# A list scheduler's table of durations: TensorE passes at traced issue times, and a shared way into SBUF for VectorE and GpSimd

## The chip, the core and the metric

One core of one Trainium2 chip runs the whole program. The metric is the device time of one execution in microseconds (us). The kernel before ran three times: 3467.73, 3470.81 and 3473.10 us, median 3470.81 us. One more execution was profiled, and all rows below are from it.

## What is computed

Two transformer blocks one after the other, all in 32-bit floats, for 512 tokens (and 256 context tokens in the first block) of width 1024:

```python
for li in range(2):                                   # the first block
    h  = half_ffn(h, ...); hc = half_ffn(hc, ...)     # h + 0.5 * gate * (silu(z @ Wg) * (z @ Wu)) @ Wd
    y, yc = even_mixer(...) if li == 0 else odd_mixer(...)   # attention beside a gMLP, or beside pooling
    h = h + m[5] * y
    h = half_ffn(h, ...)                              # and hc again in layer 0
# the second block: one projection, gated delta rule in chunks, three sliding windows, gates, output
```

`half_ffn` has an inner width of 2816, that is 22 column blocks of 128. The factors `m` come from a modulation, a product of one vector per condition with a 1024 x 9216 matrix per layer ("ada" in the program's names).

## The kernel before

Every product with full inputs is made from three TensorE passes: each operand is split into a high and a low half (`halves`: ScalarE copies the value into the narrower type, VectorE or GpSimd subtracts), and high x high, high x low and low x high are summed in one bank. In names, `whi` and `wlo` are the halves of weights, `zh` and `zl` those of the tokens, `ah` and `al` those of the activations. `raw` is a weight tile as loaded, 128 x 1024.

An FFN (`ffn`, with `gate_up`, `swiglu` and `down` in it) runs over the 22 column blocks f. For each f, gate and up of all tokens come from seven products of sums of blocks in place of eight: GpSimd makes two sums into new tiles `ws` and three in place (`raw<-raw`), ScalarE and VectorE split seven tiles of 128 x 512 (GpSimd takes the subtraction of one of them), TensorE runs 7 x 12 = 84 passes "gu", and VectorE adds the products up, multiplies gate and up and splits the result (`al`). After every second f the down projection of a pair of blocks runs (`dn`, 6 passes of 512 columns for each of 12 halves of token tiles, or of 8), and VectorE adds it to `h`. There are three FFNs with six token tiles (384 columns in a "gu" pass) and, last in the first block, one with four tiles (256 columns). In the group of column blocks before the last one, each half of a tile of `h` is also multiplied by the gate (VectorE, `h<-h,gate`) and the residual is added (GpSimd, `h<-h,hin`). At the end of an FFN or an output projection, `scaled` takes the rows' root mean square (GpSimd raises to a power: `rr<-ms`), VectorE scales (`xn<-h,rr`), TensorE transposes (`tr`), VectorE and ScalarE scale and shift (`h<-tr,mods`), and `combine` makes the sums and halves that the next FFN multiplies (`zs`, `zh`, `zl`, `zxh`, `zxl`).

The order in which each engine gets its instructions is not written by hand. `Program.record` notes every instruction with its inputs, a rank (phase, stream, place as written) and what `cost` says of it: how long it holds its engine and how much later its result is there. `Program.order` then plays a list scheduler: it keeps a clock for each of the five engines; an engine takes the first by rank among the instructions that can start at its clock (or within WAIT = 0.12 us of it, for all but TensorE); results reach another engine after the lag plus SLACK = 0.26 us, or SLACK_PE = 0.7 us for TensorE; a tile's place in its pool has to be free. Between engines, the earliest start goes next, and at equal times the engine that stands first in ENGINES (tensor, vector, scalar, gpsimd, sync). What comes out is emitted as five fixed queues: on the chip each engine works its queue in order and waits at semaphores for real inputs only. So `cost` changes no instruction and no wait, only places in the queues. Every instruction is issued from one line, the `getattr` in `emit`: L602 before, L619 in the change, so rows tell groups apart by tile names. Of `cost`, one line gives TensorE's passes with split operands:

```python
return max(n / 2400, 0.107) + 0.0027, 0.1
```

Of the kernel before, what the change touches and what calls it, by code (L numbers as in the profile page):

```python
# [175 lines left out]
class View:  # L176
    """A part of a tile: what an instruction will read or write once the tile has a place."""
# [69 lines left out]
    def cells(self):  # L247
        """The partitions and, as bits, the pieces of each that the view covers."""
# [20 lines left out]
class Slot:  # L269
    """A tile to be: its place in a pool is taken by its first instruction and given back by its last."""  # L270
# [43 lines left out]
# What the order of the instructions leaves for guesses that prove too short, in us: how much later than its inputs an  # L314
# instruction of TensorE, or one of another engine, is taken to start; and how long an engine waits for a better one.
# [3 lines left out]
# Banks of PSUM that the first stream leaves to the one behind it.  # L319
# [29 lines left out]
class Op:  # L349
    __slots__ = ("eng", "fn", "args", "kw", "key", "phase", "deps", "users", "takes", "gives", "left", "ready",  # L350
                 "cost", "lag", "n", "t")
# [12 lines left out]
def cost(eng, fn, args, kw, n):  # L364
    """About how long an instruction holds its engine, and how much later its result is there, in us."""
# [4 lines left out]
    if eng == "tensor":  # L370
        if fn == "transpose":
            return 0.109, 0.1
        lhs, rhs = args[1], args[2]
        if rhs.dtype == F32:
            c = max(4 * n / 2400, 0.213) + 0.005
            if "tile_position" in kw:
                c /= 3.8
            elif lhs.shape[-1] == 64:
                c *= 0.63
            return c, 0.1  # L380
        return max(n / 2400, 0.107) + 0.0027, 0.1
# [14 lines left out]

class Program:
    """Instructions in the order in which they are written down, each with a rank, and the order in which the engines
    are to have them: each engine takes the first by rank among those that can start."""
# [20 lines left out]
    def record(self, eng, fn, args, kw):  # L420
# [7 lines left out]
        op.cost, op.lag = cost(eng, fn, args, kw, n)  # L428
        for v, w in [(v, False) for v in ins] + [(v, True) for v in out]:
# [19 lines left out]
    def order(self):  # L449
# [50 lines left out]

        def place(o):
            r = o.ready
# [21 lines left out]
        while len(out) < len(ops):  # L524
# [18 lines left out]
            clock[o.eng] = end  # L543
            out.append(o)
# [64 lines left out]
class Net:  # L609
# [40 lines left out]
    def split(self, v, eng=None, pool=None):  # L650
        """The two parts of each v[:, i]."""
# [12 lines left out]
    def halves(self, hi, lo, x, eng=None):  # L664
        """x as the sum of two parts, each of which one pass carries."""
        self.nc.scalar.copy(hi, x)
        (eng or self.nc.vector).tensor_sub(lo, x, hi.bitcast(F32))
# [25 lines left out]
    def proj_t(self, cols, ws):  # L693
        """Tokens on partitions: the tokens of z in cols times the columns of ws."""
# [5 lines left out]
    def proj_f(self, w, t0, n):  # L700
        """Features on partitions: 128 features times n tokens of z."""
# [6 lines left out]
    def turn(self, src, n=4):  # L708
        """n blocks of 128 columns, each with its rows and columns exchanged."""
# [13 lines left out]
    def ada(self, li, n):  # L723
        self.ada_end()
        """512 columns of a layer's modulation: of half of one of its nine vectors, for both conditions. Its last steps
        are left for ada_end."""
# [67 lines left out]
    def scaled(self, h_t):  # L794
        """The halves of a tile of h, each row over its root mean square."""
# [22 lines left out]
    def park(self, i, h, xs, ab=None):  # L818
        """The scaled halves xs of pair i of the tiles of h, rows and columns exchanged, in their place; without ab,
        what ab will scale."""  # L820
# [13 lines left out]
    def park_again(self, h, half, li, ni):  # L834
        """Scales half of the rows of what waits parked, all tokens at once."""
# [8 lines left out]
    def operands(self, zx, n):  # L844
        """What the seven products of swiglu take of z, n tokens each, by parts."""
# [10 lines left out]
    # The operands that take the place of a block of z, and what each of the others sums.  # L856
# [3 lines left out]
    def blocks(self, h, t):  # L860
        """The blocks of z for pair t of the tiles that wait in h."""
# [3 lines left out]
    def plan(self, how):  # L865
        """What a string of operands, each with the letter of an engine, says."""
# [3 lines left out]
    def summed(self, z, i, eng):  # L870
        """Operand i, whole, as a sum of blocks of z: in the place of one of them, or of its own."""
# [8 lines left out]
    def combine(self, t, h, zx):  # L880
        """The operands for the tokens of the parked pair at place t."""
# [8 lines left out]
    def combine_first(self, h, zx):  # L890
        """Those of all tokens, for which the second half of the rows is scaled last."""
# [40 lines left out]
    def gate_up(self, li, which, f, how="gggggg"):  # L932
        """The seven sums of blocks of the gate's and the up's columns f, and their parts, in the order of use."""
# [19 lines left out]
    # The blocks of gate (0, 1) and up (2, 3), by halves of the tokens, that each product adds to or is taken from.  # L953
    USES = (((0, 1), (3, 1)), ((2, 1), (3, -1)), ((1, 1), (3, 1)), ((0, 1), (2, 1)), ((0, -1), (1, 1)), ((3, 1),), ((0, 1),))

    def swiglu(self, ws, z, n, ah, al, order=(1, 3, 2, 4, 0, 6, 5)):
        """silu(gate) * up for n tokens of each half, from seven products of blocks in place of eight."""
# [17 lines left out]
    def ffn(self, li, which, nt, F, hsrc, filler, on_tile, first=None):  # L975
        """hsrc + gate * swiglu(z): the sum grows in F.h."""
# [74 lines left out]
    def gelu2(self, dst, ps):  # L1051
        """Twice the gelu of ps."""
# [8 lines left out]
    def softmax(self, M, scs, widths, sink=None):  # L1061
        """exp(s - max) / sum over the parts of the scores of a pair of heads; parts are (bank of head 0, of head 1)."""
# [31 lines left out]
    def times_v(self, M, Ps, vs, dst):  # L1094
        """dst = v^T P^T for a pair of heads; vs gives v by key tile and head."""
# [153 lines left out]
    def odd_mixer(self, M, units):  # L1249
# [24 lines left out]
        def heads(c):  # L1274
            """What attention takes of half of the heads, a tile of tokens at a time."""
# [119 lines left out]
    def silu2(self, dst, y):  # L1395
        """Twice the silu of y."""
# [430 lines left out]
def at(t, nt):  # L1827
    """Where a tile of tokens is for swiglu: those of a pair at the same place of the two halves."""
# [176 lines left out]
```

## Time and profile before

| | |
|---|---|
| median of three runs | 3470.81 us |
| lowest and highest | 3467.73, 3473.10 us |
| span of the profiled execution, first to last instruction | 3465.6 us |
| the execution's own total | not listed beside its span |
| instructions | 48809 |
| TensorE (PE) busy | 3305.0 us, 95% |
| VectorE (DVE) busy | 2553.9 us, 74% |
| ScalarE (ACT) busy | 1406.0 us, 41% |
| GpSimd (POOL) busy | 1321.4 us, 38% |
| mean DMA share | 29.3% of 16 engines |

The span is 5.2 us under the median of the runs. A busy share is an average over stages: the FFN middles, the starts and ends of FFNs, the mixers and the second block have different limits, and the table of stretches in the rows below is what tells them apart. PE's passes are pipelined, so the length of one row in a timeline is longer than the step from one pass to the next; the step is the difference of two start times.

### The profile page before, as it was taken

What the parts mean: (1) busy time and instruction counts of PE and PEld (TensorE: products, weight loads), DVE (VectorE), ACT (ScalarE), POOL (GpSimd) and SP (SyncE); (2) the same over time, 40 slices, a digit from 0 to 9 for tenths busy, and PEclk for the clock granted to TensorE, in tenths of its full rate; (3) what the DMA queues carried; (4) which work ended last, traced back from release to release, by engine and by line L of the source; (5) the groups of instructions that cost most, each with busy time, mean ns of one, the idle gap of its engine ahead of it and who ended that gap; (6) DMA issues with size and microseconds to landing.
All of it is one profiled execution on the core that took longest, in us unless ns stands there. A gap on an engine that the chain in (4) does not pass through costs nothing.

```text
span 3465.6 us, 48809 instructions
## 1 busy us (share of the span) xinstructions
PE 3305.0 (95%) x18310; PEld 2826.1 (82%) x18310; DVE 2553.9 (74%) x4229; ACT 1406.0 (41%) x2962; POOL 1321.4 (38%) x1032
## 2 busy tenths in 40 slices
PE   6999998999999999989999988998999899999999
PEld 4879997776678999858999978867888787788987
DVE  7678778767777888888887786558999976555433
ACT  4433333544343333344334334445444443234331
POOL 4334435411343444554443353116555543333000
PEclk9999999999999999999999999998999999999999
DMA  5442123231433212242122132343332341112231
GB/s 209 137 160 74 56 74 115 89 128 56 173 127 136 73 56 73 85 168 91 56 73 73 65 123 80 113 158 104 100 102 92 118 122 43 31 49 74 82 98 61
DMA packets 161532, 337.73 MB, mean 97 GB/s; under 512 B 12256, under 2 KB 57696, under 8 KB 161168
## 3 DMA queue, kind: packets, MB, share of 16 engines
q1 hardware_dynamic: 161296, 334.61, 29.3%
q8 instruction: 144, 2.36, 0.3%
q14 instruction: 92, 0.75, 0.1%
HBM read 316.69 MB, written 17.87 MB: 97 GB/s over the span
## 4 chain that ended last, share of the span: by engine, by line
PE 38%; DVE 13%; issue 2%; ACT 1%; POOL 1%; DMA 1%; SPq 0%; ACTq 0%; DVEq 0%; POOLq 0%
PE gu L602 9%; PE pj L602 8%; PE dn L602 5%; DVE wlo L602 4%; PE pjf L602 4%; DVE h L602 3%; DVE gu L602 2%; DVE al L602 2%; PE dmm L602 2%; PE dnp L602 1%; PE fin L602 1%; PE yb L602 1%; PE p L602 1%; PE tr L602 1%; PE sc L602 1%
## 5 line engine op out<-in xcount | busy, mean ns | idle before, releaser
L602 DVE TENSOR_TENSOR wlo<-raw,whi 128x512 fp32r<-128x512 f32 x797 | 670.0, 867 | 197.8 <-ACT whi L602 173.2
L602 ACT CAST whi<-raw 128x512 fp32r<-128x512 f32 x885 | 523.8, 620 | 501.5 <-DMA raw<-in_ffn_gu 116.2
L602 DVE TENSOR_TENSOR gu<-gu 128x384 f32<-128x384 f32 (+1 forms) x880 | 469.1, 564 | 211.4 <-PE gu L602 172.8
L602 POOL TENSOR_TENSOR ws<-raw 128x512 f32<-128x512 f32 x176 | 249.1, 1420 | 828.8 <-DVE gu L602 596.5
L602 ACT ACTIVATE gu<-gu 128x384 f32<-128x384 f32 (+1 forms) x528 | 242.2, 474 | 504.8 <-DVE gu L602 343.4
L602 POOL TENSOR_TENSOR raw<-raw 128x512 f32<-128x512 f32 x264 | 430.6, 1655 | 2.0 <-DVE wlo L602 0.6
L602 PE MATMUL gu<-zh,wlo 128*128 128x384 f32 (+1 forms) x1408 | 300.3, 335 | 55.7 <-DVE wlo L602 54.9
L602 PE MATMUL dn<-whi,ah 128*128 128x512 f32 x968 | 308.3, 397 | 0.2 <-DVE adaSs L602 0.2
L602 DVE TENSOR_TENSOR h<-h,dn 128x512 f32<-128x512 f32 x404 | 269.6, 679 | 52.0 <-PE dn L602 49.2
L602 PE MATMUL dn<-wlo,ah 128*128 128x512 f32 x968 | 307.8, 396 | 0.0
L602 PE MATMUL dn<-whi,al 128*128 128x512 f32 x968 | 307.5, 396 | 0.0
L602 PEld LDWEIGHTS gu<-zh,wlo 128*128 128x128 f32 x1408 | 241.0, 195 | 79.7 <-DVE wlo L602 78.7
L602 PE MATMUL gu<-zh,whi 128*128 128x384 f32 (+1 forms) x1408 | 289.5, 328 | 15.8 <-ACT zh L602 11.2
L602 PE MATMUL gu<-zl,whi 128*128 128x384 f32 (+1 forms) x1408 | 293.0, 328 | 1.2 <-DVE zl L602 1.2
L602 PEld LDWEIGHTS gu<-zh,whi 128*128 128x128 f32 x1408 | 239.9, 192 | 38.1 <-ACT zh L602 14.4
L602 POOL TENSOR_TENSOR rr<-ms,constA 128x4 f32<-128x4 f32 (+3 forms) x112 | 109.4, 980 | 377.5 <-DVE ms L602 362.2
L602 PEld LDWEIGHTS gu<-zl,whi 128*128 128x128 f32 x1408 | 241.9, 193 | 4.1 <-DVE zl L602 2.0
L602 DVE TENSOR_TENSOR wlo<-ws,whi 128x512 fp32r<-128x512 f32 x176 | 220.9, 1269 | 4.8 <-ACT whi L602 3.3
L602 PE MATMUL gu<-zxh,wlo 128*128 128x384 f32 (+1 forms) x1056 | 219.3, 327 | 3.0 <-DVE wlo L602 2.8
L602 PE MATMUL gu<-zxh,whi 128*128 128x384 f32 (+1 forms) x1056 | 214.7, 328 | 7.8 <-ACT whi L602 6.4
L602 ACT CAST whi<-ws 128x512 fp32r<-128x512 f32 x176 | 108.6, 618 | 270.7 <-PE dn L602 227.1
L602 PEld LDWEIGHTS dn<-whi,al 128*128 128x128 f32 x968 | 182.8, 189 | 42.1 <-DVE al L602 0.3
(359 smaller groups left out, 6040.6 us busy)
## 6 DMA issues: line engine op xcount, KB each, us to landing
raw<-in_ffn_gu SPq DMA_DIRECT2D x176, 512.0 KB, 5.2
raw<-in_ada_w SPq DMA_DIRECT2D x144, 512.0 KB, 4.6
raw<-in_ffn_w_down SPq DMA_DIRECT2D x88, 512.0 KB, 3.5
raw<-in_w_in SPq DMA_DIRECT2D x72, 512.0 KB, 3.7
raw<-in_od_w_in SPq DMA_DIRECT2D x16, 512.0 KB, 3.6
raw<-in_ev_w_in SPq DMA_DIRECT2D x14, 512.0 KB, 3.8
gate<-gate SPq DMA_DIRECT2D x10, 512.0 KB, 3.8
raw<-in_ev_w_out SPq DMA_DIRECT2D x8, 512.0 KB, 5.2
```

The lines of the kernel that those rows point to most:

```text
L602: getattr(self.real[o.eng], o.fn)(*[real(x) for x in o.args], **{k: real(v) for k, v in o.kw.items()})
```

## The change

A TensorE pass on split operands is planned at n / 2400 + 0.0135 us, and 0.112 us at least: 0.1735 us in place of 0.1627 for 384 columns, 0.1202 in place of 0.1097 for 256, 0.2268 in place of 0.2160 for 512. Each VectorE and GpSimd instruction gets a mark `port`: GpSimd's when it reads anything in SBUF, VectorE's when it has two whole inputs in SBUF, or is a `tensor_scalar` or `tensor_copy` from SBUF to SBUF. In the planner, marked instructions pass one after the other: one may start when the last one is done, 0.15 us sooner behind one of GpSimd's. No instruction is added, taken out or given to another engine. The rest of the diff takes out docstrings and comments.

```diff
 class Op:
     __slots__ = ("eng", "fn", "args", "kw", "key", "phase", "deps", "users", "takes", "gives", "left", "ready",
-                 "cost", "lag", "n", "t")
+                 "cost", "lag", "n", "t", "port")
...
-        return max(n / 2400, 0.107) + 0.0027, 0.1
+        return max(n / 2400 + 0.0135, 0.112), 0.1
...
+def port(eng, fn, args, kw):
+
+
+    ins = [x for x in list(args[1:]) + [v for k, v in kw.items() if k != "accum_out"]
+           if isinstance(x, View) and x.tile.space is None and (x.shape[1:] != (1,) or eng == "gpsimd")]
+    if eng == "gpsimd":
+        return bool(ins)
+    if eng != "vector" or fn in ("tensor_reduce", "reciprocal"):
+        return False
+    return len(ins) > 1 or (fn in ("tensor_scalar", "tensor_copy") and len(ins) == 1 and args[0].tile.space is None)
...
+        op.port = port(eng, fn, args, kw)
...
+        way = [0.0]
+
         def place(o):
-            r = o.ready
+            r = max(o.ready, way[0]) if o.port else o.ready
...
             end = t + o.cost
             clock[o.eng] = end
+            if o.port:
+                way[0] = end - (0.15 if o.eng == "gpsimd" else 0.0)
```

What the new durations do to the queues, at three places.

TensorE at the start of the program, from the third transposed piece of the modulation (`tr<-constA,adaSs`) to the fourth, which the second half of the first FFN's input waits for. `ada` is the modulation's product, `gu` are the first products of the first FFN. Before:

```order
L602 MATMUL ada<-raw,scp 32x512 x2
L602 MATMUL gu<-zh,whi 128x384 x3
L602 MATMUL gu<-zh,wlo 128x384 x4
L602 MATMUL gu<-zl,whi 128x384 x2
L602 MATMUL ada<-raw,scp 32x512 x2
L602 MATMUL gu<-zl,whi 128x384 x2
L602 MATMUL gu<-zxh,wlo 128x384
L602 MATMUL gu<-zxl,whi 128x384 x3
L602 MATMUL ada<-raw,scp 32x512 x2
L602 MATMUL gu<-zxl,whi 128x384
L602 MATMUL ada<-raw,scp 32x512 x2
L602 MATMUL tr<-constA,adaSs 128x128 x4
```

and in the change, the third piece in the first row:

```order
L619 MATMUL tr<-constA,adaSs 128x128 x4
L619 MATMUL gu<-zh,wlo 128x384
L619 MATMUL ada<-raw,scp 32x512 x2
L619 MATMUL gu<-zh,wlo 128x384 x3
L619 MATMUL gu<-zl,whi 128x384 x4
L619 MATMUL ada<-raw,scp 32x512 x6
L619 MATMUL tr<-constA,adaSs 128x128 x4
```

Seventeen "gu" passes stood between the third and the fourth piece (one of them, `gu<-zh,whi`, ahead of the first row shown), and now eight; ahead of the third piece, four stand in place of seven.

VectorE in the middle of the FFN with four tiles, one stretch that repeats in each pair of column blocks, from one split of activations (`al`) on. `gu<-gu` adds a product from PSUM or, at the end, multiplies two tiles in SBUF; `h<-h,dn` reads PSUM. Before:

```order
L602 TENSOR_TENSOR al<-gu,ah 128x256 x2
L602 TENSOR_TENSOR wlo<-ws,whi 128x512 x2
L602 TENSOR_TENSOR h<-h,dn 128x512
L602 TENSOR_TENSOR wlo<-raw,whi 128x512
L602 TENSOR_TENSOR gu<-gu 128x256 x4
L602 TENSOR_TENSOR wlo<-raw,whi 128x512 x4
L602 TENSOR_TENSOR gu<-gu 128x256 x5
L602 TENSOR_TENSOR h<-h,dn 128x512
L602 TENSOR_TENSOR gu<-gu 128x256
L602 TENSOR_TENSOR h<-h,dn 128x512
L602 TENSOR_TENSOR wlo<-raw,whi 128x512
L602 TENSOR_TENSOR al<-gu,ah 128x256 x2
```

and in the change:

```order
L619 TENSOR_TENSOR al<-gu,ah 128x256 x2
L619 TENSOR_TENSOR wlo<-ws,whi 128x512
L619 TENSOR_TENSOR h<-h,dn 128x512 x2
L619 TENSOR_TENSOR wlo<-raw,whi 128x512
L619 TENSOR_TENSOR wlo<-ws,whi 128x512
L619 TENSOR_TENSOR gu<-gu 128x256 x3
L619 TENSOR_TENSOR wlo<-raw,whi 128x512
L619 TENSOR_TENSOR gu<-gu 128x256
L619 TENSOR_TENSOR wlo<-raw,whi 128x512
L619 TENSOR_TENSOR h<-h,dn 128x512
L619 TENSOR_TENSOR wlo<-raw,whi 128x512
L619 TENSOR_TENSOR gu<-gu 128x256 x5
```

Where four marked instructions stood in a row behind the products (al, al, wlo, wlo), two that read PSUM now come behind the third, and the run of four `wlo` is broken up.

VectorE where the odd mixer's output projection hands over to the last FFN, around the scaling of the last token tiles (`ms`, `xn`). Before:

```order
L602 TENSOR_TENSOR otmp<-pj,gate_21653 128x512
L602 TENSOR_TENSOR ss<-ss 128x1
L602 TENSOR_SCALAR ms<-ss 128x1
L602 TENSOR_TENSOR h<-h,otmp 128x512
L602 TENSOR_TENSOR h<-h 128x512
L602 TENSOR_SCALAR xn<-h,rr 128x512 x2
L602 TENSOR_TENSOR ss<-ss 128x1
L602 TENSOR_SCALAR ms<-ss 128x1
L602 TENSOR_TENSOR h<-h 128x512
L602 TENSOR_TENSOR zl<-h,zh 128x4x128
L602 TENSOR_SCALAR xn<-h,rr 128x512 x2
L602 TENSOR_TENSOR h<-h 128x512
```

and in the change:

```order
L619 TENSOR_TENSOR ss<-ss 128x1
L619 TENSOR_SCALAR ms<-ss 128x1
L619 TENSOR_TENSOR zl<-h,zh 128x4x128
L619 TENSOR_SCALAR xn<-h,rr 128x512 x2
L619 TENSOR_TENSOR h<-h 128x512
L619 TENSOR_TENSOR wlo<-ws,whi 128x512 x2
L619 TENSOR_TENSOR zxl<-h,zxh 128x4x128
L619 TENSOR_TENSOR wlo<-raw,whi 128x512
L619 TENSOR_TENSOR zxl<-zs,zxh 128x4x128
L619 TENSOR_TENSOR wlo<-raw,whi 128x512 x4
L619 TENSOR_SCALAR xn<-h,rr 128x512 x2
L619 TENSOR_SCALAR h<-tr,mods_9014 128x2x128 x4
```

The last tile's `xn`, the second one in each piece, now stands behind a sum, seven `wlo` and two `zxl`, of which it had none between it and the `xn` before it.

## Rows read from the trace of the kernel before

**Rows 1.** The page, busy time by engine and the span in 40 slices.

```profile
PE 3305.0 (95%) x18310; PEld 2826.1 (82%) x18310; DVE 2553.9 (74%) x4229; ACT 1406.0 (41%) x2962; POOL 1321.4 (38%) x1032
...
PE   6999998999999999989999988998999899999999
```

**Rows 2.** Table of stretches: us, busy us by engine, TensorE clock, DMA share, GB/s.

```profile
2420.00:2690.00 270.00, 263.90 (x1774) 239.04 (x1773) 260.34 (x390) 130.50 (x282) 152.19 (x101) 1.00 0.29 94
1600.00:1960.00 360.00, 355.86 (x1843) 328.96 (x1843) 293.86 (x403) 137.52 (x262) 147.16 (x95) 1.00 0.20 66
2350.00:2400.00 50.00, 36.38 (x218) 31.07 (x217) 46.47 (x68) 28.12 (x57) 29.08 (x20) 0.80 0.30 98
925.00:975.00 50.00, 41.00 (x190) 27.22 (x189) 45.73 (x60) 23.13 (x46) 29.91 (x21) 0.90 0.47 157
...
24.00:75.00 51.00, 35.12 (x146) 19.00 (x145) 42.54 (x50) 23.47 (x43) 28.86 (x18) 0.83 0.56 191
```

**Rows 3.** Timeline, PE, six-tile FFN: start us, us to the group's end, passes.

```profile
408.72 0.63 PE L602 MATMUL dn<-whi,al 128*128 128x512 f32 x2
409.19 0.86 PE L602 MATMUL gu<-zh,whi 128*128 128x384 f32 x4
...
411.28 0.85 PE L602 MATMUL gu<-zh,whi 128*128 128x384 f32 x4
```

**Rows 4.** Timeline, PE, four-tile FFN.

```profile
2572.63 0.64 PE L602 MATMUL gu<-zh,whi 128*128 128x256 f32 x4
2573.11 0.64 PE L602 MATMUL gu<-zh,wlo 128*128 128x256 f32 x4
```

**Rows 5.** Groups of VectorE, 2350 to 2400 us: count, busy us, mean ns, idle before.

```profile
L602 DVE TENSOR_TENSOR wlo<-raw,whi 128x512 fp32r<-128x512 f32 x10 | 10.2, 1032 | 1.0 <-ACT whi L602 1.0
...
L602 DVE TENSOR_SCALAR xn<-h,rr 128x512 f32<-128x512 f32 x6 | 5.7, 987 | 0.7 <-POOL rr L602 0.7
...
L602 DVE TENSOR_TENSOR zl<-h,zh 128x512 fp32r<-128x512 f32 x4 | 4.5, 1131 | 0.3 <-ACT zh L602 0.3
```

**Rows 6.** VectorE, all groups of one tile, whole program: ns min/median/max.

```profile
L602 DVE TENSOR_SCALAR xn<-h,rr x76: 472/481/1616, 7.7 to 2769.4; 128x512 f32<-128x512 f32 x76
```

**Rows 7.** Timelines, VectorE and GpSimd, four-tile FFN: one shared stretch.

```profile
2566.76 2.96 DVE L602 TENSOR_TENSOR al<-gu,ah 128x256 fp32r<-128x256 f32 x2
...
2573.74 0.68 DVE L602 TENSOR_TENSOR wlo<-ws,whi 128x512 fp32r<-128x512 f32 x1
...
2566.25 4.63 POOL L602 TENSOR_TENSOR raw<-raw 128x512 f32<-128x512 f32 x3
```

**Rows 8.** Timeline, PE, at the start of the program.

```profile
36.38 1.65 PE L602 MATMUL gu<-zxh,whi 128*128 128x384 f32 x4 [2.07 <-ACT whi L602]
...
51.69 0.66 PE L602 MATMUL tr<-constA,adaSs 128*128 128x128 f32 x4
52.28 1.97 PE L602 MATMUL ada<-raw,scp 128*32 128x512 f32 x12
60.65 0.69 PE L602 MATMUL gu<-zh,whi 128*128 128x384 f32 x1 [6.40 <-ACT zh L602]
```

**Rows 9.** Timelines, VectorE and GpSimd, group before the last of an FFN.

```profile
544.68 1.29 DVE L602 TENSOR_TENSOR h<-h,gate 128x512 f32<-128x512 f32 x1
...
546.60 1.29 DVE L602 TENSOR_TENSOR h<-h,gate 128x512 f32<-128x512 f32 x1
...
544.13 1.29 POOL L602 TENSOR_TENSOR h<-h,hin 128x512 f32<-128x512 f32 x1 [0.63 <-DMA hin<-in_x]
```

**Rows 10.** Chain that ended last, two pairs of column blocks, four-tile FFN.

```profile
2554.24 3.37 PE gu L602 x24
...
2587.11 3.37 PE gu L602 x24
```

**Rows 11.** Waits of PE, 2420 to 2690 us: us in total, times, longest.

```profile
PE gu L602 <- DVE wlo L602: 5.3, 9, 1.0
```

## The prediction

> **What bounds the kernel now.** I began with the page [rows 1]. TensorE is busy 3305.0 of 3465.6 us, and VectorE 2553.9: whatever the order of the queues, some 160 us at most are there to be had, and the slices show where they lie: mostly at the first slice and in those with an 8, not spread over all.
>
> The table of stretches [rows 2] says which limit holds where. In the middle of a six-tile FFN (1600 to 1960) PE is busy 355.86 of 360 us: 4.1 us are idle, so PE is the bound and the vector engines have time. In the four-tile FFN (2420 to 2690) PE has 263.90 of 270 but VectorE 260.34: two engines are near their limits at once. At the hand-overs (2350 to 2400, 925 to 975, and the start, 24 to 75) VectorE is busy 46.47, 45.73 and 42.54 us, and PE 36.38, 41.00 and 35.12, at a clock of 0.80 to 0.90 of the full one. There VectorE is the bound.
>
> Next, is the planner's new picture true? For TensorE it is. Passes of 384 columns start 411.28 − 409.19 = 2.09 us apart in twelves, 0.174 us each; the two of 512 columns take 0.47, 0.235 each [rows 3]; those of 256 take 0.48 for four, 0.120 each [rows 4]. The new 0.1735 and 0.1202 hit, and 0.2268 is still 3% short. For the shared way it is true in part. A `wlo` on an otherwise free way takes 0.68 us; while GpSimd works on three `raw<-raw` (1.54 each), an `al` of half that width takes 1.48 [rows 7]. The `xn` has a median of 481 ns and a maximum of 1616 [rows 6], with 987 on average at a hand-over [rows 5]. So instructions do hold each other up. But the chip lets the two engines alternate instruction by instruction: in the group before the last of an FFN, VectorE's `h<-h,gate` and GpSimd's `h<-h,hin` come every 1.92 us each (546.60 − 544.68), twelve times [rows 9]. The planner gives the way to the earliest start, and to VectorE at a tie.
>
> **The change, part by part.** The sum is made against the profiled span, 3465.6 us; 5.2 us are added for the distance to the median of the runs, 3470.8.
>
> *A, the start.* PE waits 6.40 us for `zh` before 60.65, and that hangs on the modulation's fourth piece at 51.69 [rows 8]. Ahead of it the queue has 12 "gu" passes fewer (3 ahead of the third piece, 9 between the third and the fourth). The four at 36.38 took 1.65 us, 0.41 each; at the full step they would take 0.174. So it is 12 × 0.174 = 2.1 to 12 × 0.41 = 4.9 us that the chain is shorter. The passes run later, in the wait that is left. I take −4, as the row of 0.41 is in the same stretch; ends 0 (if the weights of the modulation, DMA share 0.56 [rows 2], set the piece) and −4.9.
>
> *B, the middles of the six-tile FFNs and the group before their last.* PE has 4.1 us idle in 360 [rows 2], so a truer order has next to nothing to fill. The twelve multiplications and twelve sums of the lock-step group [rows 9] now come in twos and threes, with the same work on the way. 0; ends −1.3 for one such instruction saved (1.29) in either direction.
>
> *C, the four-tile FFN.* A pair of column blocks takes 2587.11 − 2554.24 = 32.87 us [rows 10]. Its passes alone take 168 × 0.120 + 48 × 0.235 = 31.4. That leaves 1.5 us in each of 270 / 32.87 = 8.2 pairs, 12 us in all, and 5.3 of it is named: nine waits of PE on `wlo` [rows 11]. Breaking up the runs of marked instructions (al, al, wlo, wlo) lets PSUM readers go while GpSimd has the way. I take half of the 12, −6, near the 5.3 that a row shows. Ends: −12, and +9 if two more such waits of 5.3 / 9 = 0.59 come in each of eight pairs (the next `al` is late, and `dn` behind it).
>
> *D, the late scaling at the last hand-over.* The last tile's `xn` stands behind ten instructions more (a sum, seven `wlo`, two `zxl`). At 0.68 each [rows 7] that is 6.8 us, at the contested 1.131 of `zl` [rows 5] 11.3. Behind it wait the transposes, `h<-tr,mods`, `zh` and half of the last FFN's first products. But the work moved ahead is wanted as well, VectorE had no idle time to lose there (46.47 of 50), and the seven `wlo` let passes on other tokens start sooner. I take +4, a third of the upper end; ends 0 and +11.
>
> *E, less standing in the way at the hand-overs.* In 2350 to 2400 the excess over undisturbed times is 10 × (1.03 − 0.68) = 3.5 us in `wlo`, 6 × (0.99 − 0.48) = 3.1 in `xn` and 4 × (1.13 − 0.68) = 1.8 in `zl` [rows 5 to 7], 8.4 in all. The total of marked work stays; only what VectorE can do meanwhile (sums that read PSUM) saves time. With three such stretches, all of it would be −25; half as much again, where the chip alternates against the plan, +13. I take −4, a sixth of the gain, since most of VectorE's work there is marked itself.
>
> Everything else is covered: SyncE's and ScalarE's queues shift by a few places, but ScalarE is busy 1406 us and waits itself [rows 1]; mean DMA share in the stretches is 0.20 to 0.56 [rows 2].
>
> Sum: −4 + 0 − 6 + 4 − 4 = −10, 3465.6 − 10 + 5.2 = 3460.8, **3461 us**.
>
> **A rule that speaks against it.** The row says 0.174 us for 384 columns and 0.235 for 512 [rows 3]. The Trainium skill, TensorE: Matmul & The Clock Gate, section Wait — 56ns, not 53.3ns?, has back-to-back matmuls start N / 2.4 GHz plus about 2.5 ns apart, which is the old table (162.5 and 216 ns). An estimate from that page makes a six-tile pair 168 × 0.1625 + 72 × 0.216 = 42.9 us, where the row's steps make it 168 × 0.174 + 72 × 0.235 = 46.2; the trace disagrees with it for these streams, and the measurement decides.
>
> **Rivals.**
>
> *Hidden, no change: 3471.* PE sets the pace over most of the span [rows 1], A's freed time may be taken by the next wait (`zh` hangs on VectorE and ScalarE too), and what C gains D loses. For it: 95% busy. Against it: A's twelve passes stand on a chain that ends in a wait of 6.40 us [rows 8]. The same time comes out if the finer durations are no truer than the old ones, because steps in other streams are shorter than those of rows 3 and 4.
>
> The page's rule named above would make it this case; as far as the traces bear it out, that is a chance of 0.03 within it.
>
> *A larger relief: 3438.* If the lock keeps the engines out of each other's way at every hand-over, E is −25, with A −4, C −6 and D at +2: −33. For it: 987 against a median of 481 in `xn` [rows 5, 6]. Against: the chip alternates whatever the plan says.
>
> *Slower, the lock favours VectorE: 3486.* Only the planner has a lock, and at a tie VectorE comes first. GpSimd's links of the chain (`rr`, half of the `zl`, `zs`) are then placed behind whole runs of VectorE's `wlo`, and `xn` of the last tile comes late, at the last hand-over and at the start of the odd mixer: two times 11 from D's upper end. With A and half of C: 3470.8 + 22 − 4 − 3 = 3486. It decides once the last `xn` starts more than some 5 us later than its `rr` could allow: by then A's gain is spent. For it: the order puts ten instructions ahead of that `xn`, and PE is idle 13.6 of 50 us there, so nothing covers a delay [rows 2]. Against: the other hand-overs keep their `xn` in place.
>
> **How the numbers follow.** Forecast 0.40 (its own range 3450 to 3464), hidden 0.22, larger relief 0.12, slower 0.26. A measurement of this kernel can tell 0.2% from no change, 6.9 us: the forecast and the larger relief are faster, 0.52; hidden is the same, 0.22; slower 0.26. The range goes from the larger relief, 3438, to the slower case, 3486; beyond them lie half of each of these cases, about 0.19 together. Adding up all the outer ends would go farther both ways, but they don't come together.
>
> **What would show it.** A: the fourth piece starts some 4 us before 51.69, and the wait of 6.40 before the next `gu<-zh,whi` shrinks. B: PE still at 355 or more of each 360 us in the middle of a six-tile FFN. C: a pair in the four-tile FFN at about 32.1 us, and fewer than nine waits on `wlo`. D: the last `xn` of the last hand-over later by 5 to 10 us, with a wait of PE on `h` behind it of some 4 more. E: means of `wlo`, `xn` and `zl` at the hand-overs below 1032, 987 and 1131 ns. I am wrong if means and pairs are as they were (hidden), or if PE's idle time grows at 925 to 975 and 2350 to 2400 and GpSimd's `rr` or `zl` end the waits (slower).

## The result, and the profile after

The changed kernel took 3521.76 us (median of four runs, 3517.95 to 3526.43), beside 3469.27 us for the kernel before in the same session: a ratio of 1.0149, 95% interval 1.0134 to 1.0163. It is 52 us slower, and 36 us beyond the range's upper end. The profiled execution spans 3521.2 us.

The page of the changed kernel, busy times and TensorE's slices:

```profile
PE 3325.9 (94%) x18310; PEld 2843.7 (81%) x18310; DVE 2466.2 (70%) x4229; ACT 1406.5 (40%) x2962; POOL 1324.4 (38%) x1032
...
PE   6999998989989999989999988997999899999999
```

VectorE is 88 us less busy than in [rows 1], with the same 4229 instructions: they stand in each other's way less, as the lock was to bring about. The time was lost all the same.

The table of stretches answers to [rows 2], each stretch moved along with the program: four-tile FFN, six-tile FFN, last hand-over, the one before the second FFN, start.

```profile
2475.00:2745.00 270.00, 266.36 (x1798) 244.29 (x1798) 243.33 (x398) 133.34 (x285) 156.39 (x103) 0.99 0.28 94
1640.00:2000.00 360.00, 360.00 (x1874) 334.68 (x1873) 265.93 (x410) 142.08 (x266) 141.77 (x94) 1.00 0.22 70
2396.00:2446.00 50.00, 32.24 (x200) 28.30 (x199) 43.53 (x61) 26.73 (x56) 26.24 (x18) 0.76 0.26 84
965.00:1015.00 50.00, 42.16 (x202) 28.72 (x201) 38.48 (x57) 22.98 (x43) 27.83 (x20) 0.93 0.52 173
24.00:75.00 51.00, 34.99 (x182) 19.82 (x180) 44.56 (x59) 25.14 (x47) 28.08 (x17) 0.97 0.66 223
```

The two FFN rows are better than before (PE 266.36 of 270 in place of 263.90, 360.00 of 360 in place of 355.86), the last hand-over is worse (32.24 of 50 in place of 36.38).

For the whole program I paired TensorE's passes: the k-th pass of a name and shape in one trace with the k-th in the other. The median shift of those in the last 8 us of a stage (by the times of before) says how late the program is by then; the difference from stage to stage is what the stage cost. The bounds are 0, 620, 655, 855, 1080, 2010, 2345, 2440, 2700 and 3466 us. The columns: the change, durations alone (e1), the lock alone (e2), and the change with the tie turned round (e6, below), each against before:

| stage | change | e1 | e2 | e6 |
|---|---|---|---|---|
| start and first FFN | −3.0 | +7.7 | −7.4 | −8.8 |
| hand-over to the even mixer | +9.0 | +3.5 | +16.6 | +5.1 |
| even mixer | +25.2 | −1.1 | +4.6 | +14.3 |
| output projection, start of the second FFN | +9.4 | +2.4 | +9.4 | +9.7 |
| second and third FFN | −7.5 | +0.9 | −0.5 | −13.1 |
| odd mixer | +10.7 | +7.7 | +8.0 | +2.6 |
| last hand-over | +13.0 | +4.7 | +6.1 | +0.5 |
| four-tile FFN | −6.4 | −3.4 | +35.9 | −14.8 |
| end of it, second block | +4.9 | −3.4 | +15.8 | −8.7 |
| sum | +55.3 | +19.0 | +88.5 | −13.2 |

The rows of the hand-over to the even mixer and of that mixer are best read together. TensorE does other work around 655 us in these runs: by 660 us the change has run 23 `pjf` passes (projections by features) and 12 `ada` passes that the kernel before runs later, and 23 `pj` passes (projections by tokens) fewer. So the place of the bound moves time from one row to the other. Their sum is the surer number: 34.2 us in the change, 2.4 in e1, 21.2 in e2, 19.4 in e6. The expectations that give the mixer 40 us count from 655 to 990 us (6.0 us late to 46.1).

**The last hand-over.** Timelines of the changed kernel, VectorE, GpSimd and TensorE:

```profile
2405.58 0.88 DVE L619 TENSOR_SCALAR xn<-h,rr 128x512 f32<-128x512 f32 x2
2406.38 1.76 DVE L619 TENSOR_TENSOR h<-h 128x512 f32<-128x512 f32 x1
2408.06 3.43 DVE L619 TENSOR_TENSOR wlo<-ws,whi 128x512 fp32r<-128x512 f32 x2
...
2414.28 2.48 DVE L619 TENSOR_TENSOR wlo<-raw,whi 128x512 fp32r<-128x512 f32 x4
2416.69 0.87 DVE L619 TENSOR_SCALAR xn<-h,rr 128x512 f32<-128x512 f32 x2
...
2405.15 0.95 POOL L619 TENSOR_TENSOR rr<-ms,constA 128x1 f32<-128x1 f32 x1 [1.73 <-DVE ms L619]
...
2406.12 1.15 PE L619 MATMUL tr<-constA,xn 128*128 128x128 f32 x4 [4.65 <-DVE xn L619]
2417.22 3.15 PE L619 MATMUL tr<-constA,xn 128*128 128x128 f32 x12 [9.95 <-DVE xn L619]
```

The last tile's `rr` is there at 2406.10. Its `xn` starts at 2416.69, 10.6 us later, behind the ten instructions that the order puts ahead of it, and TensorE stands still for 9.95 us. With the wait ahead of it, it waits 14.6 us for `xn` here, 7.6 before (2350 to 2400 us).

**The even mixer.** Stretches of 660 to 760, 760 to 820 and 820 to 880 us, first before, then changed:

```profile
660.00:760.00 100.00, 99.09 (x659) 72.94 (x656) 67.18 (x206) 48.78 (x142) 14.74 (x15) 1.00 0.20 64
760.00:820.00 60.00, 59.69 (x424) 42.31 (x422) 42.36 (x125) 29.86 (x83) 8.09 (x6) 1.00 0.27 89
820.00:880.00 60.00, 59.99 (x380) 41.99 (x377) 47.65 (x108) 27.18 (x55) 9.96 (x8) 1.00 0.34 113
```

```profile
660.00:760.00 100.00, 97.42 (x620) 69.96 (x620) 62.26 (x185) 45.49 (x131) 12.36 (x14) 1.00 0.29 96
760.00:820.00 60.00, 43.71 (x225) 29.02 (x224) 22.56 (x74) 15.67 (x50) 2.90 (x2) 0.72 0.09 27
820.00:880.00 60.00, 58.17 (x437) 43.98 (x436) 49.38 (x129) 33.02 (x80) 11.96 (x9) 1.00 0.05 19
```

Before, attention's dependent steps lay under independent projections all the way. Now one stretch has 225 passes where there were 424, and the granted clock is 0.72 on average there, between its two levels of 1.2 and 2.4 GHz. TensorE's timeline in it (`sc` are the scores, `ptr` transposes the softmax's result `P`, `arr` holds scaled queries or keys):

```profile
769.75 1.09 PE L619 MATMUL tr<-constA,arr 128*128 128x128 f32 x4 [5.58 <-DVE arr L619]
770.77 2.50 PE L619 MATMUL sc<-kT,qT 64*128 64x256 f32 x8
775.85 2.40 PE L619 MATMUL ptr<-constA,P 128*128 128x128 f32 x10 [2.58 <-ACT P L619]
...
784.72 0.66 PE L619 MATMUL ptr<-constA,P 128*128 128x128 f32 x4 [2.28 <-ACT P L619]
...
794.26 2.40 PE L619 MATMUL ptr<-constA,P 128*128 128x128 f32 x10 [3.13 <-ACT P L619]
```

Here scores, softmax and products run one behind the other with nothing between, and after the wait of 5.58 us eight `sc` take 2.50 us, at a granted clock of 0.50; before they took 1.14, at 1.00 (TensorE, kernel before):

```profile
770.23 1.14 PE L602 MATMUL sc<-kT,qT 64*128 64x256 f32 x8
```

Part of what lay between them was spent early, and part comes late. First the passes of `pjf` in 600 to 660 and 660 to 760 us, before and after; then those of `pj` in 760 to 820 us, before and after:

```profile
600.00:660.00 60.00, 0.00 (x0) 0.94 0.44 152
660.00:760.00 100.00, 38.03 (x192) 1.00 0.20 64
```

```profile
600.00:660.00 60.00, 6.51 (x23) 0.94 0.51 175
660.00:760.00 100.00, 33.05 (x169) 1.00 0.29 96
```

```profile
760.00:820.00 60.00, 23.49 (x90) 1.00 0.27 89
```

```profile
760.00:820.00 60.00, 8.47 (x35) 0.72 0.09 27
```

The same 192 `pjf` passes are done in both by 760 us. In the change they are done by 740 us, when before 53 were still to come, and 23 of them stand at the start of the mixer. Attention's own steps are behind: 80 `sc` are done by 760 us, 104 before. Of `pj`, about as many are done by then as before (271 and 264), but then none runs from 764 to 814 us, and 35 fall in the stretch that had 90. Why the order leaves them out there was not settled.

### The profile page after: what moved, and what is told of

Same layout as the page of the kernel before. It is cut to its first block, busy times and chain, and to the rows that moved or that the text cites. A ratio compares the mean times of both kernels' runs of the same rounds, so it can differ in the third digit from the quotient of the medians.

```text
span 3521.2 us, 48913 instructions
## 1 busy us (share of the span) xinstructions
PE 3325.9 (94%) x18310; PEld 2843.7 (81%) x18310; DVE 2466.2 (70%) x4229; ACT 1406.5 (40%) x2962; POOL 1324.4 (38%) x1032
## 5 line engine op out<-in xcount | busy, mean ns | idle before, releaser
L619 DVE TENSOR_TENSOR wlo<-raw,whi 128x512 fp32r<-128x512 f32 x797 | 633.9, 817 | 215.8 <-ACT whi L619 200.4
L619 DVE TENSOR_TENSOR gu<-gu 128x384 f32<-128x384 f32 (+1 forms) x880 | 450.6, 544 | 248.7 <-PE gu L619 206.4
L619 POOL TENSOR_TENSOR raw<-raw 128x512 f32<-128x512 f32 x264 | 408.0, 1564 | 17.7 <-DVE wlo L619 11.4
L619 PE MATMUL gu<-zh,whi 128*128 128x384 f32 (+1 forms) x1408 | 287.8, 327 | 19.9 <-ACT whi L619 15.3
L619 PEld LDWEIGHTS dn<-whi,ah 128*128 128x128 f32 x968 | 180.7, 189 | 52.4 <-ACT ah L619 13.3
L619 DVE TENSOR_TENSOR wlo<-ws,whi 128x512 fp32r<-128x512 f32 x176 | 196.3, 1118 | 29.6 <-ACT whi L619 28.7
```

The source lines that it names most:

```text
L619: getattr(self.real[o.eng], o.fn)(*[real(x) for x in o.args], **{k: real(v) for k, v in o.kw.items()})
```

## The experiments

The theories at the outset. **L**: the lock makes the loss, by placing GpSimd's and VectorE's links late. **D**: TensorE's longer durations make it. **S**: neither; a greedy order reshuffles the mixers at any nudge. Then, from the first four runs, **T**: in the plan, the shared way and VectorE come free at the same instant (the end of VectorE's marked instruction), the tie goes to VectorE, and GpSimd's links starve behind runs of `wlo`; and against it **P**: the lock is too long whoever goes first.

**e1, durations alone.**

```diff
-        op.port = port(eng, fn, args, kw)
+        op.port = False
```

> Only TensorE's new durations, no lock. Theory L (the lock makes the loss: it places GpSimd's and VectorE's links of the mixers late, and TensorE takes its independent products too early): the gains of the FFN middles stay, the two losses (the even mixer, 40 us, and the last hand-over, 12 us) go: 3440 to 3455 us. Theory D (the durations make it: TensorE's clock in the plan is 6 per cent slower against the other engines): 3500 us or more, with the idle stretch of TensorE in the even mixer. Theory S (any nudge reshuffles the mixers): the mixer differs from both, by 10 us or more either way, and the hand-over too.

Measured: 3488.74 us, ratio 1.0053 (1.0038 to 1.0067). Neither L's nor D's number, and the mixer does not move by S's 10 us. The even mixer is whole (−1.1), so D falls as the cause there; but the durations alone lose 7.7 us up to the end of the first FFN, 7.7 in the odd mixer and 4.7 at the last hand-over, and gain 3.4 in the four-tile FFN.

**e2, lock alone.**

```diff
-        return max(n / 2400 + 0.0135, 0.112), 0.1
+        return max(n / 2400, 0.107) + 0.0027, 0.1
```

> Only the lock, TensorE's old durations. Theory L: 3515 to 3535 us, the losses of the whole change with less of its gain in the FFN middles. Theory D: 3455 to 3475 us. Theory S: some other value, with the mixer off by 10 us or more either way.

Measured: 3557.36 us, 1.0243 (1.0225 to 1.0261), worse than all expected. The lock loses at each hand-over, and 35.9 us in the four-tile FFN, where the whole change gains. Waits of TensorE in that FFN, 2495 to 2760 us of e2:

```profile
PE dn L619 <- ACT ah L619: 12.0, 6, 2.0
PE dn L619 <- DVE gu L619: 5.9, 7, 0.8
```

There `dn` stands in TensorE's queue and waits for activations. That passes behind it could have run meanwhile is likely, but not shown.

**e3, no marks in the even mixer.**

```diff
-        op.port = port(eng, fn, args, kw)
+        op.port = port(eng, fn, args, kw) and self.phase != 2
```

> The whole change, but nothing is marked in the even mixer's phase (projections, attention, gMLP), so the lock holds in all other phases. Theory L: the 40 us of the even mixer come back, 3475 to 3490 us, and the last hand-over stays 12 us late. Theory D: the mixer keeps its loss, 3510 to 3525 us. Theory S: in between, with another order in the mixer.

Measured: 3497.64 us, 1.0078 (1.0063 to 1.0093), between L's case and D's, as S had it. The mixer's row is 4.4 us in place of 25.2, but that of the hand-over ahead of it (part of the FFN's phase) is 16.2 in place of 9.0. Together they are 20.6 in place of 34.2: the mixer's own marks make 13.6 of it, the rest comes without them.

**e4, a nudge to the kernel before.**

```diff
-SLACK = 0.26
+SLACK = 0.27
```

> The kernel before with one number nudged: SLACK 0.27 in place of 0.26 us, no other edit. It measures how far any change of the planner's numbers moves the time. Theories L and D: within 0.3 per cent of before, 3460 to 3480 us, the even mixer within 5 us. Theory S: the mixers or hand-overs move by 10 us or more, in sum 3485 us or above or 3455 us or below.

Measured: 3472.60 us, 1.0005 (0.9996 to 1.0015). Single stages move by up to 9 us (+5.2 from 990 to 1570 us, −8.9 from there to 2010) and cancel; the even mixer moves by 1.5. S as the whole explanation falls, but a shift of up to 9 us in a single stage of a single run explains nothing.

**e5, `rr` unmarked.**

```diff
     if eng == "gpsimd":
-        return bool(ins)
+        return bool(ins) and kw.get("op") != OP.pow
```

> The whole change, but GpSimd's power instruction (rr, inputs of 1 to 8 columns) carries no mark, so in the plan it never waits for the way. Theory T (at a tie VectorE gets the way, so rr is planned late and xn or qn behind it stand late in VectorE's queue): the last xn of the last hand-over follows its rr at once again, the 13 us lost from 2345 to 2440 us fall to 3 or less, and the links of the mixers come earlier too: 3475 to 3500 us in all. Theory P (the lock is too pessimistic whoever goes first, and the loss is in all marked work, not in rr): 3510 to 3530 us.

Measured: 3492.18 us, 1.0061 (1.0046 to 1.0076). The total is T's, its place is not: the even mixer falls to 5.8 us (7.1 with the hand-over ahead of it), but the last hand-over still loses 10.4. Its last `xn` does follow `rr` at once, and TensorE's waits for `xn` there are 7.0 us in all, about as before. Waits on VectorE's `wlo` (3.6) and ScalarE's `whi` (2.7) come behind them instead; what makes these was not settled.

**e6, GpSimd first at a tie.** One condition more in the choice of the next instruction:

```diff
-                if pick and (best is None or pick[0] < best[0]):
+                if pick and (best is None or pick[0] < best[0] or (pick[0] == best[0]
+                        and e == "gpsimd" and best[2].port and pick[2].port)):
```

> The whole change, but where a marked GpSimd and a marked VectorE instruction could start at the same time, GpSimd goes first, so that the plan lets the two alternate as the chip does. Theory T: GpSimd's rr, zl and zs all come in time: 3465 to 3495 us, with the last hand-over as before. Theory P: the length of the lock is unchanged, 3510 to 3530 us.

Measured: 3454.27 us, 0.9952 (0.9938 to 0.9967): from 52 us slower to 17 us faster by a rule for ties, faster even than T had it. The last hand-over in e6, VectorE, GpSimd, TensorE:

```profile
2371.30 2.80 DVE L619 TENSOR_SCALAR xn<-h,rr 128x512 f32<-128x512 f32 x4
2374.03 0.68 DVE L619 TENSOR_TENSOR h<-h 128x512 f32<-128x512 f32 x1
...
2371.47 0.75 POOL L619 TENSOR_TENSOR rr<-ms,constA 128x1 f32<-128x1 f32 x1 [0.29 <-DVE ms L619]
...
2371.84 1.15 PE L619 MATMUL tr<-constA,xn 128*128 128x128 f32 x4 [5.06 <-DVE xn L619]
2373.77 1.11 PE L619 MATMUL tr<-constA,xn 128*128 128x128 f32 x4 [0.78 <-DVE xn L619]
```

All four `xn` of the last two tiles run together, and TensorE's second wait is 0.78 us in place of 9.95. In the four-tile FFN of e6 both engines are about as busy as in the changed kernel (TensorE 266.36, VectorE 243.33 there), with 50 more passes in the same 270 us:

```profile
2418.00:2688.00 270.00, 266.83 (x1848) 247.75 (x1847) 244.83 (x410) 135.31 (x290) 152.13 (x104) 1.00 0.31 100
```

**e7, marks in the FFNs' middles alone.** A flag that is true in the FFN's loop, and false in `on_tile`, `filler` and `ada_end`:

```diff
-        op.port = port(eng, fn, args, kw)
+        op.port = self.middle and port(eng, fn, args, kw)
```

> TensorE's new durations everywhere, marks only on what the middles of the FFNs record (sums, splits, products, down projections), none in hand-overs, mixers and the second block. If the gains of the FFN middles (some 16 us in the whole change) come from the marks there and the losses from marks elsewhere: 3470 to 3480 us, the durations alone (3489) less 10 to 16 us. If the marks' gain depends on marks elsewhere: 3485 to 3500 us.

Measured: 3469.46 us, 0.9997 (0.9987 to 1.0006): as before, just under the first case. Marks in the middles give back what the durations alone lose (19.3 us to e1), and the even mixer's loss is gone (−0.7). The odd mixer's is not: 14.8 us, with nothing marked in it.

**e8, durations too in the middles alone.** As e7, and:

```diff
-        return max(n / 2400 + 0.0135, 0.112), 0.1
+        return (max(n / 2400 + 0.0135, 0.112) if middle else max(n / 2400, 0.107) + 0.0027), 0.1
```

> Marks and new durations only on what the middles of the FFNs record, all else planned as before. If each edit pays only where its engines are near their limits: 3450 to 3462 us, before less the 16 us of the FFN middles, as the mixers keep their order. If a new clock in the FFNs reshuffles what follows anyway: 3475 us or more.

Measured: 3459.30 us, 0.9964 (0.9951 to 0.9977), within the first case. VectorE still wins ties here: where only the FFNs' middles are marked, that makes no loss against the kernel before.

**e9, GpSimd first, the even mixer planned as before** (phase 2), on top of e6.

```diff
-        op.cost, op.lag = cost(eng, fn, args, kw, n)
-        op.port = port(eng, fn, args, kw)
+        op.cost, op.lag = cost(eng, fn, args, kw, n, self.phase != 2)
+        op.port = self.phase != 2 and port(eng, fn, args, kw)
```

where the last argument of `cost`, if false, stands for the old line of durations.

> As e6 (GpSimd first at a tie), but in the even mixer's phase neither marks nor new durations. In e6 that mixer (655 to 990 us of before's time) still lost 26 us against before, most of it given back later. If the marks or durations there cost that: 3430 to 3445 us. If the loss only moved (it is made up before the next FFN ends) or comes with the changed start of the phase: 3450 to 3460 us.

Measured: 3447.12 us, 0.9938 (0.9923 to 0.9953), between the two cases. The mixer still costs 8.5 us, though its own numbers are those of before, and with the hand-over it costs 18.3, about e6's 19.4. So that loss comes in with the state that the work ahead of the mixer leaves.

**e10, GpSimd first, marks and durations in the middles alone** (e8's flag with e6's rule).

```diff
+        op.port = self.middle and port(eng, fn, args, kw)
...
+                        and e == "gpsimd" and best[2].port and pick[2].port)):
```

> As e8 (marks and new durations on what the FFNs' middles record alone), with GpSimd first at a tie. Theory T in the middles: GpSimd's sums come in time, and the four-tile FFN gains 15 us as in e6 in place of 9: 3445 to 3455 us. If ties matter only where rr, zl and zs are marked: as e8, 3456 to 3463 us.

Measured: 3453.46 us, 0.9956 (0.9942 to 0.9970). The four-tile FFN gains 15.4 us in place of e8's 8.7, as T has it. But the hand-over to the even mixer and the mixer cost 21.6 us together, where e8 has 0.9: turning the tie round in the FFNs' middles alone is enough to bring that loss in.

**e11, GpSimd first and `rr` unmarked** (e6 with e5's line).

```diff
-        return bool(ins)
+        return bool(ins) and kw.get("op") != OP.pow
```

> As e6, and rr without a mark. If an rr that waits for the way in the plan still costs where VectorE's instruction came first: 3440 to 3450 us. If the tie was the whole matter: as e6, 3450 to 3460 us.

Measured: 3474.33 us, 1.0013 (1.0004 to 1.0023): 20 us slower than e6, a miss for both cases. The last hand-over (+0.5) and the four-tile FFN (−14.9) are e6's; the even mixer costs 20.1 us and the odd one 9.8. So the mark on `rr` gains 20 us with GpSimd first and costs 30 with VectorE first (e5), most of it in the hand-over to the even mixer and that mixer: single marks can move this kernel by that much.

**e12, GpSimd first, old durations** (e6 with e2's line).

```diff
-        return max(n / 2400 + 0.0135, 0.112), 0.1
+        return max(n / 2400, 0.107) + 0.0027, 0.1
```

> As e6, with TensorE's old durations: the lock alone with GpSimd first at a tie. In the lock alone with VectorE first (3557 us) the four-tile FFN lost 36 us to before, where TensorE waits on ScalarE's and VectorE's activations ahead of dn. If that comes from TensorE's passes planned too short at 256 columns: the FFN still loses 25 us or more, 3480 to 3500 us. If it comes from the tie: it gains 5 to 15 us as in e6, 3450 to 3470 us.

Measured: 3483.26 us, 1.0042 (1.0027 to 1.0057). The four-tile FFN gains 15.5 us, so e2's loss of 35.9 there needs VectorE first at the tie; it needs the old durations too, for the change, with VectorE first and the new ones, gains 6.4. The total is still above the range given for that case, since the hand-over to the even mixer and the mixer lose 29.5 together, and the second block (from 2700 us on) 15.3, as in e2 with the same durations.

**e13, the tie turned round in the even mixer only; e14, everywhere but there.**

```diff
-                        and e == "gpsimd" and best[2].port and pick[2].port)):
+                        and e == "gpsimd" and best[2].port and pick[2].port and pick[2].key[0] == 2)):
```

(`!= 2` in e14)

> The whole change, with GpSimd first at a tie only in the even mixer's phase. If the tie inside that mixer makes its 25 us: they fall to 10 or less, and all else stays, 3498 to 3510 us. If the mixer's loss comes from the state in which the hand-over leaves it: still 20 us or more there, 3515 to 3530 us.

> The whole change, with GpSimd first at a tie everywhere but in the even mixer's phase. If the tie inside the mixer makes its loss: 20 us or more are lost there, but the last hand-over and the FFNs gain as in e6, 3465 to 3485 us. If it comes from outside: the mixer loses 10 us or less, 3450 to 3460 us.

Measured: e13 3511.65 us, 1.0119 (1.0104 to 1.0134), the mixer at 20.6, so the total is between the two cases and the mixer in the second; e14 3455.29 us, 0.9954 (0.9939 to 0.9969), the mixer at 16.0. The tie inside that mixer is worth 10 us in e13's total and 1 in e14's (beside e6). Turned round everywhere else, it brings 66 of the 67 us by which e6 is faster than the change; the mixer's loss shrinks when what comes before is planned better, but doesn't go.

**e15, as e9, and the odd mixer planned as before too.**

```diff
-        op.port = self.phase != 2 and port(eng, fn, args, kw)
+        op.port = self.phase not in (2, 4) and port(eng, fn, args, kw)
```

(and so for the durations)

> As e9, with neither marks nor new durations in the odd mixer's phase either. If marks cost in that mixer as well: 3438 to 3445 us. If not, as e9: 3445 to 3452 us.

Measured: 3445.49 us, 0.9933 (0.9915 to 0.9951): the lowest of all, 24 to 26 us under the kernel before. It is at the edge between the two cases, and with e9 inside each other's intervals, so it doesn't show that marks cost in the odd mixer.

**The tie in one view.** Cost of two stages against before, in all runs with marks there, by who goes first:

| | last hand-over | four-tile FFN |
|---|---|---|
| VectorE first: change, e2, e3, e5, e13 | +13.0, +6.1, +13.4, +10.4, +12.0 | −6.4, +35.9, −5.7, −6.2, −6.4 |
| VectorE first, marks in FFN middles only: e7, e8 | +4.0, +2.2 | −8.9, −8.7 |
| GpSimd first: e6, e9, e11, e12, e14, e15 | +0.5, +2.2, +0.5, +0.5, +0.4, +0.5 | −14.8, −15.2, −14.9, −15.5, −15.1, −15.1 |
| GpSimd first, marks in FFN middles only: e10 | +1.8 | −15.4 |

With the rest equal, turning the tie round is worth 67 us with the new durations (change and e6), 74 with the old ones (e2 and e12), 18 with `rr` unmarked (e5 and e11) and 6 where only the FFNs' middles are changed (e8 and e10). Of the 68 us between the sums of the change and e6, 21 lie at the two places of this table, 15 in the hand-over to the even mixer and that mixer, 14 in the last stage; the rest is spread.

## Why the prediction was wrong

*A, right in the queue, less in the end.* The fourth piece came 4.8 us earlier (51.69 to 46.85), the pass behind the wait 4.1 us earlier (60.65 to 56.58), and the wait was 2.94 in place of 6.40 [rows 8]. It is the lock that does it, not TensorE's new durations: the fourth piece is at 46.12 in e2 and at 52.47 in e1. By the pairing, 1.7 us of the gain are left at 250 us. TensorE at the start of the changed kernel:

```profile
46.85 0.66 PE L619 MATMUL tr<-constA,adaSs 128*128 128x128 f32 x4
...
56.58 0.96 PE L619 MATMUL gu<-zh,whi 128*128 128x384 f32 x4 [2.94 <-ACT zh L619]
```

*B, too small.* I gave the six-tile middles 0. TensorE took all of the 4.1 us that lay idle in 360: PE 360.00. Over the stretches 250 to 560, 1080 to 1430 and 1570 to 1950 the program gains 3.8, 1.6 and 5.2 us, 10.6 in all. How much of that the change makes is open: the nudge of e4 gives 1.1, 0.8 and 6.8 in the same stretches.

*C, right.* A pair of column blocks takes 2646.64 − 2614.77 = 31.87 us, forecast about 32.1; the stage gains 6.4, forecast 6; waits on `wlo` fell from nine to two (no more from 2475 us on, a stretch as long as that of [rows 11]). The chain that ended last, and the waits of 2500 to 2745 us:

```profile
2614.77 2.14 PE gu L619 x16
...
2646.64 2.14 PE gu L619 x16
```

```profile
PE gu L619 <- DVE wlo L619: 0.7, 2, 0.5
```

*D, the mechanism right, the size wrong.* "I take +4, a third of the upper end" was 13.0, above even that end of 11.3. The ten instructions took 10.3 us (2406.38 to 2416.69), as bounded, but nothing covered them: "the seven `wlo` let passes on other tokens start sooner" did not happen, since TensorE's queue has the transposes of that `xn` next and no such pass ahead of them. What makes up the rest was not traced; the granted clock of the stretch was 0.76, 0.80 before.

*E, the sign.* The contested instructions did get shorter, as forecast. The groups of VectorE from 2396 to 2446 us, beside [rows 5]:

```profile
L619 DVE TENSOR_TENSOR wlo<-raw,whi 128x512 fp32r<-128x512 f32 x9 | 8.0, 921 | 0.0
...
L619 DVE TENSOR_TENSOR zl<-h,zh 128x512 fp32r<-128x512 f32 x4 | 2.6, 679 | 0.0
...
L619 DVE TENSOR_SCALAR xn<-h,rr 128x512 f32<-128x512 f32 x4 | 1.7, 476 | 0.0
```

`xn` at 476 ns and `zl` at 679 are undisturbed. But of E's three stretches only the start gained time: the last hand-over cost 13.0, and from 925 to 1080 us the change lost 2.1. An instruction that runs undisturbed after the work that it releases was due is no gain. I priced the excess and not the order that avoids it.

*The step that failed most* is "Everything else is covered". The two mixers had no term: the hand-over into the even one and that mixer cost 34.2 us together, and the odd mixer's stage 10.7. All that stood against it was "the other hand-overs keep their `xn` in place" and that PE sets the pace over most of the span. But a stage in which TensorE is busy 99% of the time has its dependent chain covered by independent passes in that order only. The stretches of the even mixer above show it: 424 passes in 60 us before, 225 in the change.

*The rivals.* "Slower, the lock favours VectorE" had the right sign and the right cause: with the tie turned round (e6) the loss is gone. It had a chance of 0.26. One of its two places is right, the last hand-over (13.0 us, beside 11). At the start of the odd mixer, from 2010 to 2130 us, the change lost 3.5; the 6.4 that follow up to 2200 us come with the durations alone (6.2 in e1) and with GpSimd first (6.1 in e6) too. Its 3486 lacked the even mixer and the hand-over into it, 34 us. Of the chances, the objection "the other hand-overs keep their `xn` in place" weighed too much. "Only the planner has a lock" holds of the program, which emits no wait for it; on the chip the two engines do take turns. The row from which I read that, [rows 9], does not show it by itself, since each sum there adds to the half tile that the multiplication has just written, and so has to wait for it. [rows 7] does: three `raw<-raw` and two `al` have no data in common, and each `al` ends 0.3 us behind one of the `raw<-raw`, about 1.5 us apart.

That the new durations might be no truer than the old ones, within the case "hidden", is refuted by the steps: over the whole program before, the median step between passes of one kind without a wait is 0.174 us for 384 columns, 0.120 for 256 and 0.227 to 0.237 for 512. By this, the trace disagrees with the rule of the Trainium skill (TensorE: Matmul & The Clock Gate, Wait — 56ns, not 53.3ns?) that I weighed, N / 2.4 GHz plus about 2.5 ns, for these streams. Truer durations need not make a better order: alone they cost 18 us (e1), with the lock they are worth 36 (e2 against the change) and 29 (e12 against e6).

*Open:* why the even mixer costs what it does. Read with the hand-over ahead of it, it costs 0.9 to 2.4 us in e1, e7 and e8, where nothing outside the FFNs' middles is marked and VectorE goes first; 17.7 to 21.6 in e3, e9, e10 and e15, which mark nothing in it either; and 7.1 to 34.2 where it is marked (the change, e2, e5, e6, e11 to e14). So its own marks are not needed for the loss, and turning the tie round takes 15 us of it away and leaves 19.4. It is a stretch without cover, in e6 too (262 passes from 740 to 800 us, at a clock of 0.80); which early decision of the planner leads there was not settled, and for this stage S, a reshuffle by small causes, stands. Of the durations alone (e1) the loss of 7.7 us up to the end of the first FFN was not followed up either.

## What to carry to other kernels

A resource that a planner hands out needs the chip's rule for taking turns, not only its exclusion: with the same lock, "VectorE at a tie" cost 52 us and "GpSimd at a tie", by which the plan lets the two alternate, as the trace does [rows 7], gained 17. When the order of queues changes, look in each stage that runs at full occupancy for what covers its dependent chain, and price the loss of that cover; and first put a new rule only where its engines are at their limit, as here the FFNs' middles (−13 us with the tie as it was, e8).

## What the runs showed of the hardware

A stall costs again in the clock. In the 60 us of the even mixer where TensorE waited, its granted clock was 0.72 on average; behind a wait of 5.58 us it was 0.50, the level of 1.2 GHz, and eight score passes took 2.50 us in place of 1.14 at 1.00. And how much VectorE and GpSimd stand in each other's way does not set the time by itself: VectorE was busy 2553.9 us before, 2466.2 in the change and 2423.2 in e15, and the time went up by 52 us in the one and down by 26 in the other. The page of e15:

```profile
PE 3293.1 (96%) x18310; PEld 2826.0 (82%) x18310; DVE 2423.2 (70%) x4229; ACT 1412.3 (41%) x2962; POOL 1321.2 (38%) x1032
```
